# A float32 transformer block on one core: the mixer's triangular inverses in lockstep, its stick-breaking heads in pairs

## The chip, the cores and the metric

One core of a Trainium2 chip runs the whole program. The metric is the time of one execution in microseconds (us) on the device. The engines are PE (TensorE; PEld is its weight load), DVE (VectorE), ACT (ScalarE), POOL (GpSimd) and SP (SyncE, which here only issues DMAs).

## The reference

Two blocks of a model run one after the other on 256 tokens of width 1024, in float32: first attention and a gated feed-forward net, then a hybrid mixer and a mixture of 32 experts. The change lies in the hybrid mixer, which has two branches. One is a gated delta rule over chunks, four heads of 128:

```python
a = jnp.where(strict, jnp.einsum("bhnid,bhnjd->bhnij", k_beta, k) * lmask, 0.0)
m = a + jnp.eye(c, dtype=a.dtype)
u = lax.linalg.triangular_solve(m, v_beta, left_side=True, lower=True, unit_diagonal=True)
w = lax.linalg.triangular_solve(m, k_beta * jnp.exp(decay)[..., None], left_side=True, lower=True, unit_diagonal=True)
...
def step(state, inp):
    qd, kd, uc, wc, qkc, cd = inp
    v_new = uc - jnp.einsum("bhcd,bhde->bhce", wc, state)
    o = jnp.einsum("bhcd,bhde->bhce", qd, state) + jnp.einsum("bhij,bhje->bhie", qkc, v_new)
    state = state * cd[..., None, None] + jnp.einsum("bhcd,bhce->bhde", kd, v_new)
    return state, o
```

The other is stick-breaking attention, eight heads of 64 (each query row sees the 16 meta tokens and the tokens before it):

```python
z = jnp.einsum("bhqd,bhkd->bhqk", q[:, :, s0:s1], k[:, :, :s1]).astype(jnp.float32) * scale
log_keep = jnp.where(mask, jax.nn.log_sigmoid(-z), 0.0)
later = lax.cumsum(log_keep, axis=3, reverse=True) - log_keep
weights = jnp.where(mask, jnp.exp(jax.nn.log_sigmoid(z) + later), 0.0)
outs.append(jnp.einsum("bhqk,bhkd->bhqd", weights.astype(v.dtype), v[:, :, :s1]))
```

Both branches are projected, gated, added and projected again; after a layer norm the experts follow.

## The kernel before

Two kinds of work share PE. The first is the weight stream (class Stream): all dense products of the model in 316 units, in a fixed order. A unit is 128x512 weights, split by ACT into a high part (tiles hiA, hiB) and by DVE into the rest (loA, loB), both in a float32r form, and then 12 products with the high and low parts of the activations (tile fm in the mixer). Up to 7 units are split ahead. Units can have a gate that must be open. The second kind is threads: Python generators for everything that isn't a dense product (attention, norms, the mixer's two branches). All their matmuls are in float32, and each of these leaves two PE instructions; a transpose leaves one.

The order on every engine is written out when the program is built. The function drive() keeps a clock of its own for each engine, with a price for each instruction (classes Queue and TensorQueue, whose calls all have the lines 176, 208 and 213 in the profile). As long as the products issued in the last 0.85 us of that clock hold fewer than WANT = 1000 columns, it takes the next piece of the stream; else the thread whose next step is due; if none is due, the stream again. A stream piece can say that it can't go on (feed() returns False), and the stream then stands until it can. On the chip every engine runs its list in order.

The mixer's part begins at some 380 us. Its threads:

- dn_prep(ci) for the chunks ci = 1, 2 (128 rows) and 0 (16 rows) makes the decays E, the triangular matrix AT, the products PT, and the scaled v and k (vp, ktok).
- dn_inv(ci), one thread for each chunk, inverts the triangular matrix by doubling, in two diagonal blocks of 64 rows for the large chunks: at each level l a masked part am of the matrix (made by POOL), Y = am x (half of the columns), an ACT copy, Z = XD Y, a DVE subtraction from X, and then turned(): four heads' transposes, the lower block by PE's transpose and the upper one by a product with the identity, and an ACT copy to XD. Five levels for the large chunks, three for the small one; at the end one off-diagonal block (YL, Z).
- state_thread runs the three chunks in order (KS, w, Su, QS, PW) when their inverses and preparations are there, and o_thread ends each.
- sb_thread runs the stick-breaking heads. sb_head makes the scores (sz, 64 rows of contraction, 144 and 272 columns), three ACT passes, a DVE pass and two scans, a POOL subtraction, an ACT pass, five transposes (swt), copies; two heads share the products with v (sav). It waits for "sv0" to "sv3", which the stream's value units finish through sv_emit.
- cut_thread starts six loads of expert weights when the heads and the inverses have ended: their tiles lie in the same memory (cut). Nearly all the tiles of both branches are views of it, so the profile calls them cut.

Buffers of limited number are given out by the class Turns: a buffer can be taken when the one taken as many turns before has been given back. d2_turns has 5 (E, dsq, sv, R, w and others); a value unit of the stream waits for one of them (room in win_tiles and fm_tile). When all threads have ended, drive() returns, the mixer's memory is closed, further expert slots are opened, and the stream goes on with the gate br0.

Of the kernel before, what the change touches and what calls it, by code (L numbers as in the profile page):

```python
# [17 lines left out]
D = 1024  # L18
# [29 lines left out]
WANT = 1000.0  # L48
LNS = 1.0
# [131 lines left out]
class TensorQueue:  # L181
# [4 lines left out]
    def __init__(self, clock, engine):  # L186
        self.clock, self.engine, self.now = clock, engine, 0.0
        self.past, self.recent = [], 0.0
# [12 lines left out]
    def matmul(self, out, w, x, **k):  # L201
# [126 lines left out]
def build(tc, I, out):  # L328
# [35 lines left out]
    with ExitStack() as ctx:  # L364
# [62 lines left out]
        d2_turns, z_turns, w_turns, m_turns, p_turns = Turns(5), Turns(3), Turns(2), Turns(3), Turns(2)  # L427
# [1107 lines left out]
        def dn_prep_thread():  # L1535
# [35 lines left out]
            for ci in (1, 2, 0):  # L1571
                spawn(dn_prep(ci))
            spawn(state_thread())
            yield

        def dn_prep(ci):
# [18 lines left out]
            for h in range(4):  # L1595
                T.matmul(p[:C, h * C:(h + 1) * C], kdT[:, h, sl], kdT[:, h, sl], start=True, stop=True)
            X_["AT"] = iv.tile([C, 4, C], F32, name="AT%d" % ci)
            for h in range(4):
                V.scalar_tensor_tensor(X_["AT"][:, h], p[:C, h * C:(h + 1) * C], fb_[:C, ci, h:h + 1], E[:C, h], op0=OP.mult, op1=OP.mult)
            V.tensor_mul(fs[:C, ci], fb_[:C, ci], E[:C, :, C - 1])  # L1600
            if not full:
                d2_turns.give(nE)
            spawn(dn_inv(ci))
            yield
            if full:
                p = acc_tile("kq")
                for h in range(4):
                    T.matmul(p[:C, h * C:(h + 1) * C], kdT[:, h, sl], qdT[:, h, sl], start=True, stop=True)
                X_["PT"] = dm.tile([128, 4, C], F32, name="PT%d" % ci)
                for h in range(4):  # L1610
                    V.scalar_tensor_tensor(X_["PT"][:C, h], p[:C, h * C:(h + 1) * C], fb_[:C, ci, h:h + 1], E[:C, h], op0=OP.mult, op1=OP.mult)
                d2_turns.give(nE)
                yield
            pv = acc_tile("vtp")
            for h in range(4):
                T.transpose(pv[:C, h * 128:(h + 1) * 128], M["raw3"][2][:, h, sl], ident)
            X_["vp"] = (dm if full else iv).tile([128 if full else 16, 4, 128], F32, name="vp%d" % ci)
# [3 lines left out]
            yield  # L1621
            if full:
# [3 lines left out]
                p = acc_tile("qtp")  # L1626
                for h in range(4):
                    T.transpose(p[:C, h * 128:(h + 1) * 128], qdT[:, h, sl], ident)
                for h in range(4):
                    A.activation(sq[:C, h], v4(p)[:C, h], AF.Square, accum_out=fq[:C, ci, h:h + 1])  # L1630
# [6 lines left out]
        def dn_inv(ci):  # L1637

            t0, C = CH[ci]
            X_ = DNC[ci]  # L1640
            AT = X_["AT"]
            K = min(C, 64)
            blocks = [slice(b, b + K) for b in range(0, C, K)]
            L = 4 if C == 16 else 6
            XT = (dm if ci else iv).tile([C, 4, C], F32, name="XT%d" % ci)
            XX = iv.tile([C, 4, K], F32, name="XX%d" % ci)
            bc = lambda t: t[:C, None, :K].to_broadcast([C, 4, K])
            if C > K:
                D_ = iv.tile([C, 4, K], F32, name="AD%d" % ci)
                XD = iv.tile([C, 4, K], F32, name="XD%d" % ci)  # L1650
                for b in blocks:
                    A.copy(D_[b], AT[b, :, b])
                G.memset(XT[K:, :, 0:K], 0.0)
            else:
                D_, XD = AT, XT

            def masked(l):
                am = iv.tile([C, 4, K], F32, name="am%d" % ci, tag="am%d" % ci)
                G.tensor_mul(am, D_, bc(lmask[:, l]))
                return am  # L1660

            def turned():
                p = acc_tile("xt")
                for h in range(4):
                    x = (XX if l else XD)[:, h]
                    T.transpose(p[:K, h * K:(h + 1) * K], x[:K], ident[:K, :K])
                    if C > K:
                        T.matmul(p[K:C, h * K:(h + 1) * K], x[K:], ident[K:C, K:C], start=True, stop=True)
                return v4(p, K)

            l = 0
            yield
            am = masked(0)
            yield
            V.tensor_sub(XD, bc(identc), am)
            am = masked(1)
            yield
            p = turned()
            A.copy(XX, p[:C])
            yield  # L1680
            for l in range(1, L):
                m = 1 << l
                H = K // 2
                xl = XX.rearrange("p h c -> p (h c)").rearrange("p (x u m) -> p x u m", u=2, m=m)[:, :, 0]
                xh = XX.rearrange("p h (x u m) -> p h x u m", u=2, m=m)[:, :, :, 0]
                p = acc_tile("Y")
                for h in range(4):
                    for b in blocks:
                        T.matmul(p[b, h * H:(h + 1) * H], am[b, h], xh[b, h], start=True, stop=True)
                Y = iv.tile([C, 4, H], F32, name="Y%d" % ci, tag="Y%d" % ci)  # L1690
                A.copy(Y, v4(p, H)[:C])
                if l < L - 1:
                    am = masked(l + 1)
                yield
                p = acc_tile("Z")
                for h in range(4):
                    for b in blocks:
                        T.matmul(p[b, h * H:(h + 1) * H], XD[b, h], Y[b, h], start=True, stop=True)
                V.tensor_sub(xl, xl, p[:C, :4 * H].rearrange("p (x m) -> p x m", m=m))
                yield  # L1700
                p = turned()
                if l < L - 1 or C == K:
                    A.copy(XD, p[:C])
                else:
                    A.copy(XT[blocks[0], :, blocks[0]], p[blocks[0]])
                    V.tensor_copy(XT[blocks[1], :, blocks[1]], p[blocks[1]])
                yield
            if C > K:
                lo, hi = blocks
                p = acc_tile("Y")  # L1710
                for h in range(4):
                    T.matmul(p[hi, h * K:(h + 1) * K], AT[lo, h, hi], XX[lo, h], start=True, stop=True)
                Y = iv.tile([C, 4, K], F32, name="YL%d" % ci, tag="am%d" % ci)
                A.copy(Y[hi], v4(p, K)[hi])
                yield
                p = acc_tile("Z")
                for h in range(4):
                    T.matmul(p[lo, h * K:(h + 1) * K], Y[hi, h], XT[hi, h, hi], start=True, stop=True)
                A.mul(XT[lo, :, hi], v4(p, K)[lo], -1.0)
                yield  # L1720
            X_["XT"] = XT
            finish("inv%d" % ci)
# [107 lines left out]
        def sb_thread():  # L1830
            for pr in range(4):
                yield from wait("sv%d" % pr)
                yield from sb_pair(pr)
            finish("sb")

        def sb_head(pr, hh, us):
            skT, sqT = M["skT"], M["sqT"]
            b = hh * 64
            yield from room(z_turns, 2 * pr + hh)
            nz = z_turns.take()  # L1840
            p = a_tile("sz")
            for a in range(2):
                T.matmul(p[:, ZS[a]], sqT[b:b + 64, pr, a * 128:(a + 1) * 128], skT[b:b + 64, pr, :144 + 128 * a],
                         start=True, stop=True)
            z = sw.tile([128, 416], F32, "z", "z%d" % (nz % 3))
            l = sw.tile([128, 416], F32, "l", "l%d" % (nz % 3))
            V.tensor_add(z, p[:, :416], smask)
# [6 lines left out]
            for a in range(2):  # L1854
                r = l[:, ZS[a]][:, ::-1]
                V.tensor_tensor_scan(r, ones.to_broadcast([128, 144 + 128 * a]), r, 0.0, OP.mult, OP.add)
            yield
            G.tensor_sub(z, z, l)
# [3 lines left out]
            yield from room(w_turns, 2 * pr + hh)  # L1862
            nw = w_turns.take()
            pt = acc_tile("swt")
            pt2 = a_tile("swt2")
            for a in range(2):
# [635 lines left out]
```

## Time and profile before

| | |
|---|---|
| time before, median of 3 runs | 861.77 us (850.72, 861.77, 868.59) |
| profiled execution, its own time | 868.72 us |
| its span, first to last instruction | 867.0 us |
| PE, PEld busy | 835.1 us (96%), 693.1 us (80%) |
| DVE, ACT, POOL busy | 489.1 us (56%), 410.5 us (47%), 66.0 us (8%) |
| read from memory | 184.99 MB, 215 GB/s over the span |
| mean granted clock | 0.919 |

The busy time of PE has modelled ends, and matmuls overlap, so the price of one is read from the distance of two starts. Times in the rows are from the span's start. The granted clock is 1.00 at 2.4 GHz and 0.50 at 1.2 GHz.

### The profile page before, as it was taken

How to read it: one execution, taken by the hardware profiler on the slowest of the kernel's cores; microseconds unless marked ns; L12 is line 12 of the kernel's file. 1: busy time of each engine (PE TensorE's matmuls, PEld its weight loads, DVE VectorE, ACT ScalarE, POOL GpSimd, SP SyncE). 2: the span in 40 equal slices, each digit the busy share in tenths (PEclk: the TensorE clock that was granted, in tenths of full speed). 3: DMA queues.
4: the chain of work that ended last, by engine and by line, in shares of the span. 5: the costliest groups of instructions: out<-in, count | busy, mean ns of one | idle time of the engine just before them, and what ended most of it. 6: DMA issues, size and time to landing. Idle time of an engine off the chain costs nothing. (4 is left out here: it accounts for less than half of the span.)

```text
span 867.0 us, 17005 instructions
## 1 busy us (share of the span) xinstructions
PE 835.1 (96%) x6775; PEld 693.1 (80%) x6775; DVE 489.1 (56%) x1245; ACT 410.5 (47%) x903; POOL 66.0 (8%) x99
## 2 busy tenths in 40 slices
PE   8999999999999999999999999999999999998985
PEld 7888899999999999899776767999986555545532
DVE  7676658998788888998332323575655131131104
ACT  6555557765566666766422323575534121222101
POOL 0000001000000002342210101000310000000001
PEclk9999999999999999999855555999999999988998
DMA  8533544474565452754110101399498999999992
GB/s 290 159 117 128 154 147 147 152 239 146 163 226 165 177 195 98 278 164 143 50 49 1 49 1 49 132 410 391 137 340 308 384 423 426 421 425 425 423 403 99
DMA packets 93971, 187.15 MB, mean 216 GB/s; under 512 B 10490, under 2 KB 71219, under 8 KB 82499
## 3 DMA queue, kind: packets, MB, share of 16 engines
q1 hardware_dynamic: 93731, 185.78, 58.6%
q8 instruction: 54, 0.88, 0.4%
q14 instruction: 26, 0.21, 0.1%
q10 hardware_dynamic: 160, 0.27, 0.1%
HBM read 184.99 MB, written 1.05 MB: 215 GB/s over the span
## 5 line engine op out<-in xcount | busy, mean ns | idle before, releaser
L208 PE MATMUL fm<-ah,hiB 128*128 128x256 f32 x268 | 77.4, 289 | 0.0
L208 PE MATMUL fm<-al,hiB 128*128 128x256 f32 x268 | 75.6, 282 | 0.0
L208 PE MATMUL fm<-ah,loB 128*128 128x256 f32 x268 | 75.2, 281 | 0.0
L176 DVE TENSOR_TENSOR hd<-small,ph 128x256 f32<-128x256 f32 x8 | 3.4, 422 | 115.7 <-ACT small L176 115.7
L208 PE MATMUL fm<-hTh,hiB 128*128 128x256 f32 (+1 forms) x184 | 61.2, 333 | 2.0 <-ACT cut L176 1.3
L208 PE MATMUL fm<-ah,hiA 128*128 128x256 f32 x212 | 61.3, 289 | 0.6 <-ACT hiA L176 0.6
L208 PE MATMUL fm<-ah,loA 128*128 128x256 f32 x212 | 59.9, 283 | 0.5 <-DVE loA L176 0.5
L208 PE MATMUL fm<-al,hiA 128*128 128x256 f32 x212 | 59.9, 282 | 0.0
L208 PE MATMUL fm<-hTl,hiB 128*128 128x256 f32 (+1 forms) x184 | 56.4, 307 | 0.0
L208 PE MATMUL fm<-hTh,loB 128*128 128x256 f32 (+1 forms) x184 | 56.4, 306 | 0.0
L208 PEld LDWEIGHTS fm<-ah,hiB 128*128 128x128 f32 x268 | 50.5, 188 | 3.1 <-issue 2.8
L208 PEld LDWEIGHTS fm<-al,hiB 128*128 128x128 f32 x268 | 50.5, 188 | 0.1
L208 PEld LDWEIGHTS fm<-ah,loB 128*128 128x128 f32 x268 | 50.5, 189 | 0.0
L176 ACT ACTIVATE small<-ph 128x256 f32<-128x256 f32 x8 | 3.1, 384 | 95.1 <-PE ph L208 95.1
L208 PE MATMUL fm<-hTh,hiA 128*128 128x256 f32 (+1 forms) x136 | 43.5, 320 | 1.1 <-ACT hiB L176 1.1
L208 PEld LDWEIGHTS fm<-hTh,hiB 128*128 128x128 f32 x184 | 38.1, 207 | 7.3 <-issue 3.6
L176 DVE SCALAR_TENSOR_TENSOR c<-u,pc,c 128x256 f32<-128x256 f32 x88 | 42.5, 483 | 1.8
L208 PEld LDWEIGHTS fm<-ah,hiA 128*128 128x128 f32 x212 | 40.4, 190 | 3.0 <-issue 1.5
L208 PE MATMUL fm<-hTl,hiA 128*128 128x256 f32 (+1 forms) x136 | 41.0, 302 | 0.8 <-DVE hTl L176 0.7
L208 PEld LDWEIGHTS fm<-ah,loA 128*128 128x128 f32 x212 | 40.4, 191 | 0.7 <-DVE loA L176 0.7
L208 PE MATMUL fm<-hTh,loA 128*128 128x256 f32 (+1 forms) x136 | 40.6, 299 | 0.0
L208 PE MATMUL ph<-xg,xe 128*32 128x256 f32 x448 | 38.8, 408 | 1.9 <-DMA xg<-in_expert_w_gate_dram 1.9
(554 smaller groups left out, 2449.6 us busy)
## 6 DMA issues: line engine op xcount, KB each, us to landing
xg<-in_expert_w_gate_dram SPq DMA_DIRECT2D x24, 1024.0 KB, 19.6
xd<-in_expert_w_down_dram SPq DMA_DIRECT2D x18, 1024.0 KB, 19.5
xu<-in_expert_w_up_dram SPq DMA_DIRECT2D x16, 1024.0 KB, 13.9
cut<-in_expert_w_up_dram SPq DMA_DIRECT2D x15, 1024.0 KB, 14.9
wg<-in_ffn_w_up_dram SPq DMA_DIRECT2D x11, 1024.0 KB, 5.1
wu<-in_ffn_w_up_dram SPq DMA_DIRECT2D x11, 1024.0 KB, 4.9
wdn<-in_ffn_w_down_dram SPq DMA_DIRECT2D x11, 1024.0 KB, 5.6
wgt<-in_w_in_dram SPq DMA_DIRECT2D x8, 1024.0 KB
```

What stands on the lines that cost most here:

```text
L176: return f(*args, **k)
L208: return self.engine.matmul(out, w, x, **k)
```

## The change

- The three threads dn_inv become one, inverse_thread. It waits for all three matrices (AT0, AT1, AT2) and copies the diagonal blocks of chunks 1 and 2 into D_, a d2 buffer that it holds to its end. Class Blocks: "J" has eight blocks of 64 for each half of the rows (two chunks, four heads), "0" the 16-row chunk. All levels run in lockstep: Y for all, copies by ACT and DVE, the next mask by DVE, then Z and ZT (the same product transposed, g.y as weights and g.xt moving) and two subtractions, from x and from its transpose xt. Y, Z and ZT have all 64 columns. No transposes are left but the first, a product with the identity.
- dn_prep computes PT in the step of AT, and the q transposes with the v transposes.
- sb_head and the old sb_pair become one thread for two heads: z and l are 2 x 416 wide, the scores of the two heads alternate, ACT's passes and DVE's take both heads at once, the subtraction z - l goes from POOL to DVE. z_turns has 2 pairs, l_turns 1, w_turns 1.
- The planner counts 0.13 us (TURN) for a change between float32 and stream products, 0.0115 for 0.0025 us per stream product, half price for paired scores, and asks for 1300 columns (MIX_WANT) while the mixer's last drive() runs.

```diff
+MIX_WANT = 1300.0
+TURN = 0.13
...
     def run(self, cost, columns, outs, ins):
+        fast = ins[0].dtype != F32
+        if fast != self.fast:
+            cost += TURN
+            self.fast = fast
         self.clock.run(self, cost, outs, ins)
...
-        return self.recent < WANT
+        return self.recent < self.want
...
-            half = 2 if r <= 64 and m <= 64 else 1
+            half = 2 if pair or (r <= 64 and m <= 64) else 1
             self.run(max(n, m) / 600 / half + 0.01, 2 * n * r / 128 / half, [out], [w, x])
         else:
-            self.run(n / 2400 + 0.0025, n * r / 128, [out], [w, x])
+            self.run(n / 2400 + (0.0115 if x.dtype == F32R else 0.0025), n * r / 128, [out], [w, x])
...
-        d2_turns, z_turns, w_turns, m_turns, p_turns = Turns(5), Turns(3), Turns(2), Turns(3), Turns(2)
+        d2_turns, z_turns, l_turns, w_turns, m_turns, p_turns = Turns(5), Turns(2), Turns(1), Turns(1), Turns(3), Turns(2)
...
+            spawn(inverse_thread())
             spawn(state_thread())
...
-        def dn_inv(ci):
...
+        class Blocks:
+            def __init__(self, name, K, halves, n, levels, d):
+                self.K, self.n, self.levels, self.d = K, n, levels, d
+                self.rows = K * halves
+                self.halves = [slice(b * K, (b + 1) * K) for b in range(halves)]
+                self.x, self.xt, self.y = (iv.tile([self.rows, n, K], F32, name=t + name) for t in ("X", "XD", "Y"))
...
+            def mask(self, l):
+                self.am = iv.tile([self.rows, self.n, self.K], F32, name="am" + self.name, tag="am" + self.name)
+                V.tensor_mul(self.am, self.d, self.bc(lmask[:, l]))
+            def each(self, p, w, x):
+                for i in range(self.n):
+                    for b in self.halves:
+                        T.matmul(p[b, i], w[b, i], x(b, i), start=True, stop=True)
+        def inverse_thread():
+            XT = dm.tile([128, 2, 4, 128], F32, name="XT")
+            G.memset(XT[64:, :, :, 0:64], 0.0)
+            lo, hi = slice(0, 64), slice(64, 128)
+            yield from room(d2_turns)
+            nD = d2_turns.take()
+            D_ = d2("D").rearrange("p a (b c) -> p (a b) c", b=2)
+            for ci in (1, 2):
+                yield from wait("AT%d" % ci)
+                for b in (lo, hi):
+                    A.copy(D_[b, 4 * ci - 4:4 * ci], DNC[ci]["AT"][b, :, b])
+            yield from wait("AT0")
+            B = [Blocks("J", 64, 2, 8, 6, D_), Blocks("0", 16, 1, 4, 4, DNC[0]["AT"])]
+            for g in B:
+                g.mask(0)
+            yield
+            P = []
+            for g in B:
+                P.append(g.psum("xt"))
+                g.each(P[-1], g.am, lambda b, i, g=g: identc[b, :g.K])
+            for g, p in zip(B, P):
+                V.tensor_sub(g.xt, g.bc(identc), g.am)
+                g.mask(1)
+                V.tensor_sub(g.x, g.bc(identc), p)
+            yield
+            for l in range(1, 6):
+                P = []
+                for g in B:
+                    P.append(g.psum("Y"))
+                    g.each(P[-1], g.am, lambda b, i, g=g: g.x[b, i])
+                for g, p in zip(B, P):
+                    if g.n == 8:
+                        A.copy(g.y[:, 0:4], p[:, 0:4])
+                        V.tensor_copy(g.y[:, 4:8], p[:, 4:8])
+                    else:
+                        A.copy(g.y, p)
+                    if l < g.levels - 1:
+                        g.mask(l + 1)
                 yield
+                P = []
+                for g in B:
+                    if g.n == 8:
+                        P.append((g.psum("Z"), g.psum("ZT")))
...
+                    g.each(P[-1][0], g.xt, lambda b, i, g=g: g.y[b, i])
+                    g.each(P[-1][1], g.y, lambda b, i, g=g: g.xt[b, i])
+                for g, (pz, pt) in zip(B, P):
+                    V.tensor_sub(g.x, g.x, pz)
+                for g, (pz, pt) in zip(B, P):
+                    if l < 5:
+                        V.tensor_sub(g.xt, g.xt, pt)
...
+            d2_turns.give(nD)
...
+        def sb_pair(pr):
             skT, sqT = M["skT"], M["sqT"]
             nz = z_turns.take()
+            yield from room(l_turns, pr)
+            nl = l_turns.take()
+            z = sw.tile([128, 2, 416], F32, "z", "z%d" % (nz % 2))
+            l = sw.tile([128, 2, 416], F32, "l", "l")
+            P = [a_tile("sz") for hh in range(2)]
             for a in range(2):
+                for hh in range(2):
+                    b = hh * 64
+                    T.matmul(P[hh][:, ZS[a]], sqT[b:b + 64, pr, a * 128:(a + 1) * 128], skT[b:b + 64, pr, :144 + 128 * a],
+                             pair=True, start=True, stop=True)
+            for hh in range(2):
+                V.tensor_add(z[:, hh], P[hh][:, :416], smask)
             yield
             A.activation(l, z, AF.Abs)
             A.activation(l, l, AF.Exp, scale=-1.0)
             A.activation(l, l, AF.Ln, bias=1.0)
             yield
             V.scalar_tensor_tensor(l, z, 0.0, l, op0=OP.max, op1=OP.add)
+            for hh in range(2):
+                for a in range(2):
+                    r = l[:, hh, ZS[a]][:, ::-1]
+                    V.tensor_tensor_scan(r, ones.to_broadcast([128, 144 + 128 * a]), r, 0.0, OP.mult, OP.add)
+            V.tensor_sub(z, z, l)
+            l_turns.give(nl)
...
+        T.want = MIX_WANT
         drive(lambda: not threads and "o2" in done and "sb3" in done)
+        T.want = WANT
```

## Rows read from the trace of the kernel before

**Rows 1.** The page's 40 slices: busy tenths of PE, tenths of the granted clock.

```profile
PE   8999999999999999999999999999999999998985
...
PEclk9999999999999999999855555999999999988998
```

**Rows 2.** Windows view: length, then busy us (instructions) per engine, clock, DMA share, GB/s.

```profile
380.00:425.00 45.00, 43.36 (x383) 39.31 (x381) 33.31 (x99) 26.41 (x91) 9.97 (x18) 1.00 0.38 118
425.00:545.00 120.00, 119.61 (x743) 88.92 (x742) 34.75 (x75) 39.74 (x94) 13.57 (x16) 0.50 0.09 27
545.00:577.00 32.00, 32.00 (x276) 31.13 (x275) 21.62 (x60) 21.89 (x58) 0.00 (x0) 1.00 0.66 264
...
720.00:760.00 40.00, 38.20 (x406) 20.82 (x398) 5.37 (x15) 8.14 (x18) 0.00 (x0) 1.00 1.01 423
```

**Rows 3.** Waits view, 425 to 545 us: who waited for whom, us, times, longest.

```profile
POOL cut L176 <- PE Y L208: 57.8, 8, 15.7
...
PEld Z L208 <- DVE cut L176: 0.7, 2, 0.5
```

**Rows 4.** Timeline of PE at full clock, 411 to 422 us: start, us, instruction.

```profile
411.98 0.24 PE L213 MATMUL xt<-ident,cut 64*64 64x64 f32 x1
...
412.41 0.24 PE L213 MATMUL xt<-ident,cut 64*64 64x64 f32 x1
...
414.50 0.65 PE L208 MATMUL Y<-cut 64*64 64x32 f32 x16
415.08 0.39 PE L208 MATMUL fm<-hTh,hiA 128*128 128x272 f32 x1
...
415.56 0.28 PE L208 MATMUL fm<-hTh,hiA 128*128 128x272 f32 x1
415.68 0.29 PE L208 MATMUL fm<-hTl,hiA 128*128 128x272 f32 x1
...
420.33 0.97 PE L208 MATMUL sz<-cut 64*128 64x144 f32 x4
421.23 0.39 PE L208 MATMUL fm<-hTh,hiA 128*128 128x272 f32 x1
```

**Rows 5.** Timeline at half clock, 440 to 449 us.

```profile
440.95 0.43 PE L208 MATMUL fm<-hTl,hiB 128*128 128x272 f32 x1
...
441.18 0.43 PE L208 MATMUL fm<-hTh,loB 128*128 128x272 f32 x1
...
442.21 1.75 PE L208 MATMUL sz<-cut 64*128 64x144 f32 x4
...
443.90 0.59 PE L208 MATMUL fm<-hTh,hiB 128*128 128x272 f32 x1
...
444.88 0.31 PE L213 MATMUL xt<-ident,cut 64*64 64x64 f32 x1
...
445.52 0.31 PE L213 MATMUL xt<-ident,cut 64*64 64x64 f32 x1
...
447.74 1.06 PE L208 MATMUL Z<-cut 64*64 64x32 f32 x16
...
448.74 0.59 PE L208 MATMUL fm<-hTh,hiB 128*128 128x272 f32 x1
```

**Rows 6.** Groups of PE by shape, 425 to 545 us: busy us, mean ns, idle before.

```profile
L213 PE MATMUL xt<-ident,cut 64*64 64x64 f32 x36 | 11.2, 310 | 0.0
...
L208 PE MATMUL Z<-cut 64*64 64x32 f32 x144 | 9.8, 293 | 0.4 <-DVE cut L176 0.4
L208 PE MATMUL Y<-cut 64*64 64x32 f32 x128 | 8.5, 294 | 0.0
...
L208 PE MATMUL Y<-cut 64*64 64x64 f32 x16 | 2.2, 318 | 0.0
```

**Rows 7.** Groups of DVE by shape, 380 to 577 us.

```profile
L176 DVE TENSOR_TENSOR_SCAN cut<-ones,cut 128x272 f32<-128x272 f32 x8 | 5.6, 699 | 0.0
...
L176 DVE TENSOR_TENSOR loB<-wz,hiB 128x512 fp32r<-128x512 f32 x5 | 3.5, 698 | 0.0
```

More of the change, by code (lines that the diff above doesn't have):

```diff
@@ L1596, in dn_prep @@
                 T.matmul(p[:C, h * C:(h + 1) * C], kdT[:, h, sl], kdT[:, h, sl], start=True, stop=True)
+            if full:
+                p2 = acc_tile("kq")
+                for h in range(4):
+                    T.matmul(p2[:C, h * C:(h + 1) * C], kdT[:, h, sl], qdT[:, h, sl], start=True, stop=True)
             X_["AT"] = iv.tile([C, 4, C], F32, name="AT%d" % ci)
@@ L1599, in dn_prep @@
                 V.scalar_tensor_tensor(X_["AT"][:, h], p[:C, h * C:(h + 1) * C], fb_[:C, ci, h:h + 1], E[:C, h], op0=OP.mult, op1=OP.mult)
+            finish("AT%d" % ci)
             V.tensor_mul(fs[:C, ci], fb_[:C, ci], E[:C, :, C - 1])
[L1601 to L1604, printed above, removed]
             if full:
-                p = acc_tile("kq")
-                for h in range(4):
-                    T.matmul(p[:C, h * C:(h + 1) * C], kdT[:, h, sl], qdT[:, h, sl], start=True, stop=True)
                 X_["PT"] = dm.tile([128, 4, C], F32, name="PT%d" % ci)
                 for h in range(4):
-                    V.scalar_tensor_tensor(X_["PT"][:C, h], p[:C, h * C:(h + 1) * C], fb_[:C, ci, h:h + 1], E[:C, h], op0=OP.mult, op1=OP.mult)
-                d2_turns.give(nE)
-                yield
+                    V.scalar_tensor_tensor(X_["PT"][:C, h], p2[:C, h * C:(h + 1) * C], fb_[:C, ci, h:h + 1], E[:C, h], op0=OP.mult, op1=OP.mult)
+            d2_turns.give(nE)
+            yield
             pv = acc_tile("vtp")
@@ L1616, in dn_prep @@
                 T.transpose(pv[:C, h * 128:(h + 1) * 128], M["raw3"][2][:, h, sl], ident)
+            if full:
+                pq = acc_tile("qtp")
+                for h in range(4):
+                    T.transpose(pq[:C, h * 128:(h + 1) * 128], qdT[:, h, sl], ident)
             X_["vp"] = (dm if full else iv).tile([128 if full else 16, 4, 128], F32, name="vp%d" % ci)
@@ L1625, in dn_prep @@
                 sq = d2("dsq")
[L1626 removed]
                 for h in range(4):
[L1628 to L1630 removed]
+                    A.activation(sq[:C, h], v4(pq)[:C, h], AF.Square, accum_out=fq[:C, ci, h:h + 1])
                 yield
@@ L1861, in sb_head @@
             yield
-            yield from room(w_turns, 2 * pr + hh)
+            yield from room(w_turns, pr)
             nw = w_turns.take()
-            pt = acc_tile("swt")
-            pt2 = a_tile("swt2")
-            for a in range(2):
-                T.transpose(pt2[:16, a * 128:(a + 1) * 128], z[:, 144 * a:144 * a + 16], ident)
-                T.transpose(pt[:, a * 128:(a + 1) * 128], z[:, 144 * a + 16:144 * a + 144], ident)
-            T.transpose(pt[:, 256:384], z[:, 288:416], ident)
@@ L1870, in sb_head @@
-            wt = sw.tile([128, 384], F32, "wt", "wt%d" % (nw % 2))
-            A.copy(wt, pt[:, :384])
-            wm = sw.tile([16, 256], F32, "wm", "wm") if nw % 2 else wm0
-            V.tensor_copy(wm, pt2[:16, :256])
+            pm = a_tile("swm")
+            PT = []
+            for hh in range(2):
+                pt = acc_tile("swt")
+                PT.append(pt)
+                for a in range(2):
+                    T.transpose(pm[:16, hh * 256 + a * 128:hh * 256 + a * 128 + 128], z[:, hh, 144 * a:144 * a + 16], ident)
+                    T.transpose(pt[:, a * 128:(a + 1) * 128], z[:, hh, 144 * a + 16:144 * a + 144], ident)
+                T.transpose(pt[:, 256:384], z[:, hh, 288:416], ident)
@@ L1874, in sb_head @@
+            wt = [sw.tile([128, 384], F32, "wt", "wt%d" % hh) for hh in range(2)]
+            wm = rt_[:16, 0:512]
+            for hh in range(2):
+                A.copy(wt[hh], PT[hh][:, :384])
+            V.tensor_copy(wm, pm[:16])
             z_turns.give(nz)
             yield
-            us.append((hh, wt, wm, nw))
-            if len(us) == 2:
-                av = a_tile("sav")
-                for c in range(3):
-                    for h2, wt, wm, _ in us:
-                        b = h2 * 64
-                        f = (2 * pr + h2) * 64
-                        if c == 0:
-                            T.matmul(av[b:b + 64, :S], M["svm"][:, f:f + 64], wm, start=True, stop=False)
-                        elif c == 1:
-                            T.matmul(av[b:b + 64, :S], M["svt"][:, 0, f:f + 64], wt[:, :S], start=False, stop=False)
-                        else:
-                            T.matmul(av[b:b + 64, 128:S], M["svt"][:, 1, f:f + 64], wt[:, S:], start=False, stop=True)
-                for u in us:
-                    w_turns.give(u[3])
-                oh, ol = M["o"][1]
-                A.copy(oh[:, pr], av[:, :S])
-                yield
-                V.tensor_sub(ol[:, pr], av[:, :S], oh[:, pr].bitcast(F32))
-                finish("sb%d" % pr)
@@ L1897, in sb_pair @@
-        def sb_pair(pr):
-            us = []
-            for hh in range(2):
-                spawn(sb_head(pr, hh, us))
-                yield
+            av = a_tile("sav")
+            for c in range(3):
+                for hh in range(2):
+                    b = hh * 64
+                    f = (2 * pr + hh) * 64
+                    if c == 0:
+                        T.matmul(av[b:b + 64, :S], M["svm"][:, f:f + 64], wm[:, hh * 256:hh * 256 + 256], start=True, stop=False)
+                    elif c == 1:
+                        T.matmul(av[b:b + 64, :S], M["svt"][:, 0, f:f + 64], wt[hh][:, :S], start=False, stop=False)
+                    else:
+                        T.matmul(av[b:b + 64, 128:S], M["svt"][:, 1, f:f + 64], wt[hh][:, S:], start=False, stop=True)
@@ L1903, in build @@
+            w_turns.give(nw)
+            oh, ol = M["o"][1]
+            A.copy(oh[:, pr], av[:, :S])
+            yield
+            V.tensor_sub(ol[:, pr], av[:, :S], oh[:, pr].bitcast(F32))
+            finish("sb%d" % pr)
         stream.open("win")
```

132 lines of the change are left out of this document (36 added, 96 removed).

## The prediction

> **What bounds the kernel now.** I read the page's slices first [rows 1]: TensorE (PE) is busy in nearly every slice, so the share of busy time says nothing; the row to see is the granted clock, which lies at half for five slices in the middle. The windows view puts bounds to it [rows 2]: from 380 to 425 us the clock is full, from 425 to 545 it is 1.2 GHz, then full again. This is the mixer: stick-breaking heads, triangular inverses and their chunks' state, with products of the weight stream put between. In those 120 us PE is busy for 119.6 while VectorE has 34.8 and ScalarE 39.7. The waits say the same [rows 3]: other engines wait for PE, GpSimd 57.8 us for one product, while the largest wait of PE's weight load for VectorE is 0.7 us. So what sets the end of this stage is the length of PE's own queue at the slow clock, not the latency of the chains.
>
> Last, the tail: experts' weights move at 423 GB/s in the window from 720 to 760 us, with the DMA share at 1.01 [rows 2], so the end is a transfer. It doesn't hide the gain: the loads that fill the DMA begin where the mixer gives its buffers back, so the tail moves with the mixer's end. I carry the mixer's gain through at its full size.
>
> **Prices of a PE instruction, at both clocks** (start to start, since matmuls overlap). A product in full float32 leaves two instructions. A stream product takes 0.12 us at full clock (415.56 to 415.68) and 0.23 at half (440.95 to 441.18) [rows 4, 5]: halved. One head's two 64x64 transposes take 0.43 us at full (411.98 to 412.41) and 0.64 at half (444.88 to 445.52). Sixteen instructions of Y or Z, 64x64 by 64x32 with the two halves of the array in turn, take 0.58 (414.50 to 415.08) and 1.00 (447.74 to 448.74). The four scores of a head (sz) take 0.90 (420.33 to 421.23) and 1.69.
>
> **Part 1, the inverses.** Today two chunks of 128 rows each run five levels of Y, Z and a transposition. In the half-clock stretch lie 36 head-turns of 0.64 us, 23.0; 272 Y and Z instructions at 1.00 per 16, 17.0; and the closing products, 16 Y of 64 columns with 2.2 us busy and as many Z, 4.4 [rows 5, 6]. Together 44.4 us. Before 425 lie the other 12 head-turns, 5.2, and 48 instructions, 1.7: 6.9 us. The change removes all transposes and makes Y, Z and a new product ZT, each 64 columns wide: 16 + 16 + 16 products a level for both chunks, five levels, and 16 to start, which makes 256 products, 512 instructions. Their price isn't in the trace as such. If the 64 columns of weights set the pace it is that of today's pairs, 0.58 per 16, 18.6 us; if the 32 moving columns set it, twice that, 37.1. The nearest row decides: the closing Y with 64 moving columns and no partner averages 2.2/16 = 0.14 us at half clock, and two halves side by side make that 1.1 per 16, against the 1.00 measured with 32 columns. So 18.6, with 18.5 more kept for the range. The closing products halve to 2.2. The 16-row chunk has about as many small products as before and is left out. New sum at full clock: 20.8.
>
> **Part 2, the heads in pairs.** The two heads of a pair lie on different halves of the rows, and their scores now alternate between them, so that they can run side by side as Y does. Seven heads in the slow stretch cost 11.8 us, 6.3 at full clock; paired, 3.1. If they don't overlap the gain is nothing; the Y rows exclude that they lose. Transposes and products with v keep their number.
>
> **Part 3, the clock.** What PE did before it fell [rows 2, 4]: groups of 64-column transposes, 1.7 us for four heads, between few stream products. In the changed kernel the transposes are gone, the 64-wide products fill both halves, and the planner asks for more stream columns at a time (MIX_WANT 1300 for 1000) and counts 0.13 us for each change between float32 and stream products. All three push the same way, so I take the clock as held through the mixer. Then what is left of the slow stretch, 119.5 - 44.4 = 75.1, halves to 37.6, less the scores' 3.1: 34.5.
>
> **Part 4, what moves to VectorE.** Masks go from GpSimd to VectorE at twice the width, 0.70 each by the 512-wide row [rows 7]: six of them; five copies of 256 columns, 0.35 each; eleven 512-wide subtractions for ten of 128; the pairs' z minus l, four at 832 columns, 1.1 each. Net some 15 us, on top of the 33.3 + 34.8 + 21.6 = 89.7 that VectorE has from 380 to 577. That is 105 of the 125 us that will be there. In the window 380 to 425 VectorE was already at 74% with PE at 96% [rows 2], so most of it stays beside PE; but masks, subtractions and the weight stream's low halves now stand in one queue, behind a pair's scans, and the inverse's next product waits behind that. I take 8 us of PE waits; nothing is one bound, 34 (below) the other. GpSimd's side is free: its 58 us of waiting was for PE.
>
> **Part 5, the planner's new costs everywhere.** They reorder products outside the mixer too. PE there is at full clock in all but short falls and 9 tenths or more busy [rows 1]; a new order can cost or give some 4 us. I take nothing.
>
> **The sum**, on the profiled execution (868.72; its span is 867.0). From 380 to 577 it used 45.0 + 119.5 + 32.0 = 196.5 us. After: 45.0 - 6.9 - 0.4 (one head's scores) = 37.7; 34.5; 32.0; inverses 20.8: 125.0. Gain 71.5, less 8 of waits, 63.5: 805. The median shown is 861.77 and the runs differ by 18 us, which the length of the slow stretch could explain; if the clock holds, the time after doesn't depend on it, so I keep 805 and not 7 less.
>
> **Rivals.** *The clock still falls.* Then 75.1 - 5.9 = 69.2 stay, the inverses cost 32 groups of 1.00 and 4.4, and there are 37.7 + 69.2 + 36.4 + 32.0 = 175.3: 848. For it: the inverse's products are still 64 by 64, and the clock fell among such products. Against: the three edits above. A fall for part of the stage gives 815 to 848. Chance 0.2.
>
> *The stream locks and the evacuations lie open.* The inverse takes one of five d2 buffers (D_) and holds it to its end; the buffers are handed out in a ring, so after four further takes (two squares, two value tiles sv0 and sv1) the fifth, sv2, must wait, and the stream stands behind it. PE then has only the lockstep, and each of its 13 steps waits for a copy (0.35) or for masks and subtractions (0.7 each), about 1.3 us a step, 17 us, and for a pair's block on VectorE (scans of 832 columns at 0.70 per 272, 2.1, and two passes of 1.1 [rows 7]), 4.3 each, 17 for four: 34. Time 831. For it: the order of the takes in the code. Against: the lockstep may be nearly through when sv2 comes. Chance 0.15. The Trainium skill has a rule that points here: "TensorEngine Tiling (Array Packing)", section Performance Considerations, says that packing speeds up the products but not the emptying of PSUM, which may become the limit. The row of before differs for this stage: there the engine behind waited 57.8 us for PE's Y [rows 3].
>
> *Slower.* Both at once: the lock starves PE at the first levels, the clock falls, and the 34 us open at half clock: 848 + 34 = 882. It is over the 2% from 2.4 us of waiting a step on, at half clock all through. Against it: the dense stream after the lock should raise the clock again, as at 545. Chance 0.04.
>
> *The change doesn't do what it says*: the chains now wait for the slowest chunk, and the removed transposes were only filler. PE's full queue speaks against it; about 862, chance 0.04.
>
> **How the numbers follow.** Forecast 0.57, at 805 (790 to 822). Two per cent is what a measurement of this kernel can tell from no change: 844.5 and 879. Faster: 0.57 + 0.15 + most of the falling clock, 0.13: 0.85. Same 0.11, slower 0.04. Range 786 (no waits, 4 from the order, the rest shrinking by a little more than half) to 846, which takes in the partial falls, the open evacuations and the dear 64-wide products (823).
>
> **What would show it.** Right: a full clock from 380 to the mixer's end, that end near 505, no xt group but the first, 16 J instructions in about 0.6 us, the experts' loads beginning some 65 us sooner. Wrong: a half clock again in that stretch; idle PE in front of Y and Z, with VectorE the releaser; a gap in the stream between sv2 and the end of the inverse. The step that I trust least is the clock.

## The result, and the profile after

The changed kernel takes 822.75 us (median of 4, 819.50 to 829.07); the kernel before beside it 861.84 (4, 850.72 to 868.59). The ratio is 0.960 [0.948, 0.972]: faster, inside the predicted range, but 18 us above the forecast of 805. Some executions of a kernel are slower at a lower granted clock; ratios, and gains over the kernel before, leave these out here and below, so they can differ a little from the quotient of the medians, most for kernels 9 to 11, where this leaves three of the seven executions of before.

The profiled execution of after took 819.50 us, its span is 817.7 and its mean granted clock 0.978. The page's slices, PE's busy tenths and its clock, answer to [rows 1]: the five slices at half clock are gone, but PE is no longer full in the middle.

```profile
PE   8999999999999999999998789999999999998894
...
PEclk9999999999999999999999899999999999989998
```

Windows of after, with the columns of [rows 2]:

```profile
380.00:425.00 45.00, 42.84 (x494) 40.13 (x493) 38.21 (x113) 26.43 (x91) 6.32 (x13) 1.00 0.41 133
425.00:545.00 120.00, 109.11 (x1131) 98.09 (x1132) 76.11 (x161) 62.39 (x132) 0.00 (x0) 0.94 0.37 139
545.00:577.00 32.00, 31.77 (x270) 31.46 (x269) 17.40 (x29) 17.85 (x33) 4.69 (x5) 1.00 0.80 304
...
720.00:760.00 40.00, 37.05 (x309) 20.55 (x310) 5.96 (x10) 6.45 (x13) 0.00 (x0) 0.94 1.01 424
```

From 425 to 545 the clock is 0.94 where it was 0.50, PE has 1131 instructions in place of 743, and VectorE's work has more than doubled, to 76 us. PE is idle for 10.9 us, where it was for 0.4. (The last 16 us of this stretch already belong to br.)

Groups of PE by shape, the first product of the gate br; first the kernel before, then after (shortest, median and longest duration in ns, first and last start in us):

```profile
L208 PE MATMUL br<-od,hiA x32: 277/280/287, 578.4 to 589.6; 128*128 128x256 f32 x32
```

```profile
L216 PE MATMUL br<-od,hiA x32: 277/280/287, 529.3 to 540.4; 128*128 128x256 f32 x32
```

This product starts 49.1 us sooner, and the span is 49.3 us shorter. So the whole gain was made ahead of br, and the tail moved along unchanged: 288.6 us from br to the end before, 288.4 after. The profile of before is of an execution at the slow end of that kernel's times, that of after of its fastest, so the spans lie further apart than the medians (39 us).

PE's timeline of after (start, us, instruction; in brackets idle time and what ended it):

```profile
425.77 0.97 PE L216 MATMUL sz<-cut 64*128 64x144 f32 x8
426.67 0.40 PE L216 MATMUL fm<-hTh,hiA 128*128 128x272 f32 x1
...
444.29 1.15 PE L216 MATMUL Y<-cut 64*64 64x64 f32 x32
445.37 0.65 PE L216 MATMUL sav<-rt,cut 16*64 16x256 f32 x4
...
447.75 1.15 PE L216 MATMUL Z<-cut 64*64 64x64 f32 x32 [0.93 <-ACT cut L179]
448.73 1.10 PE L216 MATMUL ZT<-cut 64*64 64x64 f32 x32
...
453.80 0.28 PE L221 MATMUL swm<-ident,cut 128*16 128x128 f32 x1 [3.97 <-ACT cut L179]
...
455.03 1.97 PE L216 MATMUL Y<-cut 64*64 64x64 f32 x32
```

Both prices of PE work came out. Thirty-two instructions of 64 columns take 1.08 us (444.29 to 445.37) and 0.98 (447.75 to 448.73), 0.49 to 0.54 per 16 where [rows 4] had 0.58 for 32 columns. Two heads' scores take 0.90 (425.77 to 426.67), as one head's did.

From 449.8 to 453.8 PE does nothing. PE's next instructions are a pair's transposes (swm), which wait for ACT's exponential, and this waits for VectorE. First ACT's line, then VectorE's timeline; the inverse's two subtractions, which take Z and ZT, stand behind the same work:

```profile
452.85 0.90 ACT L179 ACTIVATE cut<-cut 128x832 f32<-128x832 f32 x1 [4.88 <-DVE cut L179]
```

```profile
448.67 1.02 DVE L179 SCALAR_TENSOR_TENSOR cut<-cut 128x832 f32<-128x832 f32 x1
449.72 2.04 DVE L179 TENSOR_TENSOR_SCAN cut<-ones,cut 128x144 f32<-128x144 f32 x4
451.79 1.02 DVE L179 TENSOR_TENSOR cut<-cut 128x832 f32<-128x832 f32 x1
452.74 0.68 DVE L179 TENSOR_TENSOR cut<-cut,Z 128x512 f32<-128x512 f32 x1
453.33 0.68 DVE L179 TENSOR_TENSOR cut<-cut,ZT 128x512 f32<-128x512 f32 x1
```

That is the block of a pair which the lock rival described, 4.1 us long against the 4.3 it counted. And the stream gives PE nothing to fill it with. Windows of after for the stream's products (fm) alone, first PE, then PEld, DVE, ACT, and clock, DMA share, GB/s:

```profile
440.00:445.00 5.00, 0.64 (x3) 0.42 (x3) 0.00 (x0) 0.00 (x0) 0.88 0.00 0
445.00:450.00 5.00, 0.00 (x0) 0.00 (x0) 0.00 (x0) 0.00 (x0) 1.00 0.02 3
450.00:455.00 5.00, 0.00 (x0) 0.00 (x0) 0.00 (x0) 0.00 (x0) 0.99 0.00 0
455.00:460.00 5.00, 0.00 (x0) 0.00 (x0) 0.00 (x0) 0.00 (x0) 0.50 0.01 3
460.00:465.00 5.00, 0.00 (x0) 0.00 (x0) 0.00 (x0) 0.00 (x0) 0.83 0.00 0
465.00:470.00 5.00, 3.04 (x18) 2.39 (x18) 0.00 (x0) 0.37 (x1) 1.00 0.65 209
```

No stream product starts from 445 to 465 us. They come back when the inverse ends (its last products start at 464.9) and gives D_ back. The stretch just behind the 4 us of idleness, 455 to 460, is at half clock.

### The profile page after: what moved, and what is told of

Its sections match the earlier page's. It is cut to its first block, busy times and chain, and to the rows that moved or that the text cites. A ratio compares the mean times of both kernels' runs of the same rounds, so it can differ in the third digit from the quotient of the medians.

```text
span 817.7 us, 17080 instructions
## 1 busy us (share of the span) xinstructions
PE 770.6 (94%) x6839; PEld 654.1 (80%) x6839; DVE 501.0 (61%) x1260; ACT 401.5 (49%) x865; POOL 46.8 (6%) x74
## 5 line engine op out<-in xcount | busy, mean ns | idle before, releaser
L216 PE MATMUL fm<-hTh,hiB 128*128 128x256 f32 (+1 forms) x184 | 55.2, 300 | 3.1 <-DVE cv L179 1.4
L216 PE MATMUL fm<-hTl,hiB 128*128 128x256 f32 (+1 forms) x184 | 52.9, 288 | 0.0
L216 PE MATMUL fm<-hTh,loB 128*128 128x256 f32 (+1 forms) x184 | 52.8, 287 | 0.0
L216 PEld LDWEIGHTS fm<-al,hiA 128*128 128x128 f32 x212 | 41.0, 193 | 0.0
L216 PE MATMUL fm<-hTh,hiA 128*128 128x256 f32 (+1 forms) x136 | 40.4, 297 | 0.1
L216 PEld LDWEIGHTS fm<-hTh,hiB 128*128 128x128 f32 x184 | 35.3, 192 | 6.0 <-issue 2.7
L216 PE MATMUL fm<-hTl,hiA 128*128 128x256 f32 (+1 forms) x136 | 38.6, 284 | 0.0
```

## The experiments

Each was timed beside the kernel before, in four groups (1 to 4, 5 to 8, 9 to 11, 12) apart from the whole change, so that across groups the ratios compare better than the times. The table gives the median time (lowest to highest), the ratio to before with its 95% interval, the first start of br and the clock from 425 to 545 us, the last two from the profiled execution. That was the fastest of the four for the whole change, 1 and 10, and the slowest for 3 and 6.

| kernel | us | ratio | br | clock |
|---|---|---|---|---|
| before | 861.84 (850.72 to 868.59) | | 578.4 | 0.50 |
| whole change | 822.75 (819.50 to 829.07) | 0.960 [0.948, 0.972] | 529.3 | 0.94 |
| 1 change, own buffer for D_ | 816.04 (813.68 to 818.36) | 0.949 [0.941, 0.958] | 524.3 | 0.94 |
| 2 inverses alone | 812.21 (808.95 to 818.27) | 0.946 [0.936, 0.955] | 521.7 | 0.97 |
| 3 pairs alone | 849.50 (846.39 to 853.07) | 0.986 [0.977, 0.995] | 564.2 | 0.62 |
| 4 planner alone | 860.05 (833.66 to 894.45) | unclear | 550.5 | 0.86 |
| 5 inverses, own buffer | 811.12 (808.23 to 814.00) | 0.940 [0.935, 0.945] | 520.2 | 0.96 |
| 6 inverses and pairs | 811.11 (810.14 to 813.68) | 0.939 [0.935, 0.943] | 521.6 | 0.93 |
| 7 inverses and planner | 807.99 (807.74 to 808.77) | 0.936 [0.932, 0.940] | 519.7 | 1.00 |
| 8 products beside the transposes | 898.20 (894.00 to 903.24) | 1.039 [1.032, 1.046] | 609.5 | 0.50 |
| 9 turned by products | 808.96 (807.85 to 809.34) | 0.943 [0.932, 0.953] | 520.5 | 0.97 |
| 10 change, 1000 columns | 820.45 (811.83 to 824.38) | 0.958 [0.946, 0.970] | 520.8 | 0.99 |
| 11 change, no turn cost | 805.22 (804.16 to 806.01) | 0.939 [0.928, 0.949] | 515.2 | 0.99 |
| 12 transposes in a row | 814.51 (811.60 to 817.84) | 0.940 [0.934, 0.945] | 528.0 | 0.93 |

**The parts alone (2, 3, 4).** Each takes one part of the diff onto the kernel before.

```diff
 # 2: inverse_thread and Blocks for dn_inv, dn_prep's new order
 # 3: sb_pair for sb_head, its turns, pair=True in the planner
 #    (its low part comes in the same step as the high part; in the change one step later)
 # 4: MIX_WANT, TURN, 0.0115
```

> The kernel before with only the inverses in lockstep (and the preparation's order that goes with it); heads one by one and the planner's numbers as before. Theory: the transposes are what let the clock fall; the half clock between 425 and 545 us shrinks to under 30 us in all, and most of the 39 us comes from this part: 825 to 838. Rival: the planner's larger demand for stream columns holds the clock; then the half clock stays over most of the mixer and only some 20 us of PE work are saved: 840 to 852.

> The kernel before with only the heads in pairs (scores alternating, one thread for two heads; the low part of the result is issued in the same step as the high part); inverses with transposes and the planner's numbers as before. Theory: the clock falls as before, since the transposes are there; the scores lose 5.9 us at half clock: 853 to 862. Rival: the pairs' wider passes free so much that the clock holds: under 840.

> The kernel before with only the planner's numbers (MIX_WANT 1300, TURN 0.13, 0.0115 for each stream product). Theory: transposes still stand in groups of 1.7 us, so the clock still falls in the mixer, perhaps for a shorter time: 845 to 862. Rival: the demand for columns is what holds the clock; then it is full over the mixer with the old inverses, the 119.5 us become some 65 and the time is 810 to 825.

The inverses alone give 812, less than expected and less than the whole change. The pairs alone give 1.4%, 12 us, and not surely 2%. The planner alone is inconclusive: its ten executions lie 60 us apart, and the profiled one (845) is among the faster. The clock tells these apart. Windows of the pairs alone, 425 to 515 us:

```profile
425.00:455.00 30.00, 30.00 (x230) 23.09 (x229) 10.40 (x22) 11.21 (x22) 1.94 (x4) 0.51 0.12 36
455.00:485.00 30.00, 29.83 (x223) 21.70 (x224) 14.03 (x25) 9.32 (x23) 3.19 (x3) 0.60 0.00 1
485.00:515.00 30.00, 30.00 (x194) 21.68 (x195) 9.52 (x18) 10.55 (x22) 0.67 (x1) 0.50 0.12 36
```

Of the kernels that keep the transposes, the pairs' keeps most of the half clock (0.62) and the planner's, in that execution, 34 of 120 us (0.86); with the new inverse it is nearly gone (0.97).

**The lock (1, 5).** The whole change, and the inverses alone, with D_ in memory of its own (that of rt_, whose other use goes back to two tiles of 16 x 256).

```diff
-            yield from room(d2_turns)
-            nD = d2_turns.take()
-            D_ = d2("D").rearrange("p a (b c) -> p (a b) c", b=2)
+            D_ = rt_[:, 0:512].rearrange("p (a c) -> p a c", a=8)
...
-            d2_turns.give(nD)
```

> The changed kernel, with the blocks D_ in memory of their own instead of one of the five d2 buffers (the meta weights wm go back to two tiles of 16x256, so two copies of 256 columns for one of 512). Theory: the ring of d2 buffers stops the stream while the inverse runs; in the changed kernel's trace no stream product lies between 445 and 465 us. Then stream products appear there, the waits of the transposes swm for ACT (4.5 us) and the three short falls of the clock up to 500 us go or shrink, and the time falls by 8 to 16 us against the changed kernel, to 807 to 815. Rival: the lockstep's own hand-overs between PE, ACT and DVE cost the time, whatever stands in the stream: within 3 us of the changed kernel's 822.8.

> The inverses in lockstep alone, with the blocks D_ in a tile of their own, so that the ring of d2 buffers can't stop the stream; old heads, old planner's numbers. In the trace of the inverses alone no stream product lies between 435 and 455 us. Theory: that gap costs as in the changed kernel, where its removal gave some 7 us: 802 to 808. Rival: the stream that isn't issued there only runs later and nothing is lost: 810 to 815.

In the whole change this gives back 6.7 us by the medians, less than the 8 expected at least; the executions don't overlap, the intervals of the ratios do. The same windows of fm show products again where there were none, if not evenly:

```profile
440.00:445.00 5.00, 2.38 (x15) 1.75 (x14) 0.00 (x0) 0.39 (x1) 1.00 0.25 52
445.00:450.00 5.00, 2.01 (x12) 1.60 (x12) 0.00 (x0) 0.30 (x1) 1.00 0.46 161
450.00:455.00 5.00, 0.02 (x1) 0.00 (x0) 0.00 (x0) 0.09 (x1) 0.79 0.01 3
455.00:460.00 5.00, 3.01 (x12) 2.62 (x12) 0.00 (x0) 0.00 (x0) 0.52 0.00 0
```

With the inverses alone the same edit gives 1 us, within the scatter, although the stream stands still there too. So the lock by itself costs nothing that can be measured. That it costs when a pair's block of 4 us falls into it would explain the 6.7 us, but isn't shown: kernel 6 below has the lock and the pairs and takes 811, and kernel 11, the whole change without two of the planner's costs, has the same lock and block and still the lowest median of all. No stream product starts there from 430 to 455 us; its window of fm, and PE's wait for the block:

```profile
430.00:455.00 25.00, 0.00 (x0) 0.00 (x0) 0.00 (x0) 0.00 (x0) 0.93 0.01 2
```

```profile
443.18 0.28 PE L221 MATMUL swm<-ident,cut 128*16 128x128 f32 x1 [3.48 <-ACT cut L179]
```

**Two parts at a time (6, 7).**

```diff
 # 6: the whole change without MIX_WANT, TURN and 0.0115
 # 7: the whole change with the old sb_head and its turns
```

> Inverses in lockstep and heads in pairs, old planner's numbers: the changed kernel without its planner part. The inverses alone gave 812.2, the whole change 822.8; something in the other two parts costs 10 us. If it is the planner's numbers: 806 to 813 here. If it is the pairs: 818 to 825.

> Inverses in lockstep and the planner's new numbers, heads one by one: the changed kernel without its pairs. If the planner's numbers cost the 10 us: 818 to 826. If it is the pairs: 808 to 814.

Either addition leaves the inverses' time as it was within the scatter, 811 and 808. Only all three together cost 11 to 15 us more by the times, and the ratios agree (0.960 against 0.939 and 0.936, with intervals that don't overlap). So it is the pairs and the planner's numbers that collide.

**Which number of the planner (10, 11).**

```diff
-MIX_WANT = 1300.0      # 10
+MIX_WANT = 1000.0
-TURN = 0.13            # 11
+TURN = 0.0
-... (0.0115 if x.dtype == F32R else 0.0025)
+... (0.0025 if x.dtype == F32R else 0.0025)
```

> The whole change, with the planner asked for 1000 stream columns in the mixer as before, not 1300. Theory (more stream products between the lockstep's steps make the inverse end later and the stream's buffers run out while it waits; together with the pairs' blocks on VectorE that is the 10 to 15 us that the whole change lies above its parts): 808 to 815, and the inverse ends before 462 us (465 in the whole change). Rival (the cost of a turn between float32 and stream products moves the order, not the wanted columns): 818 to 826, as the whole change.

> The whole change, with the planner's two new costs taken back (no 0.13 us for a turn between float32 and stream products, 0.0025 us on each stream product), the 1300 columns kept. Theory of the wanted columns: no change, 818 to 826. Rival (the costs): 808 to 815. If both this and the kernel with 1000 columns come out at 818 or above, the meeting of pairs and planner is one of order alone and stays open.

It is the costs, not the columns: without them the change takes 805.2, its four executions within 2 us, and its ratio is that of kernel 6, which has none of the planner's numbers. With 1000 columns the median stays at 820; the profiled execution of that kernel was its fastest, 811.8, so its row in the table doesn't stand for the median. My theory of the columns fell. The windows from 380 to 515 us, first of the whole change, then of the kernel without turn costs:

```profile
380.00:515.00 135.00, 122.31 (x1376) 108.77 (x1375) 98.85 (x247) 71.92 (x190) 6.32 (x13) 0.95 0.24 77
```

```profile
380.00:515.00 135.00, 126.37 (x1470) 115.02 (x1470) 101.81 (x249) 79.37 (x204) 4.34 (x9) 0.99 0.35 122
```

PE is idle for 8.6 us instead of 12.7, and the clock is 0.99 instead of 0.95, another 5.4 us of PE's time (0.04 of 135). That is 9.5 of the 14.1 us by which br starts sooner. In the other executions of the whole change the clock weighs more: its four mean clocks are 0.964 to 0.978, those of kernel 11 0.983 to 0.985. By an estimate (span times what the mean clock lacks to 1) the half clock costs 24 us on average in the one and 13 in the other, 11 of the 17.5 us between them. Why the costs leave such an order with pairs and not with single heads stays open.

**What lets the clock fall (8, 9, 12).** All three are the kernel before with an edit in turned(). Kernel 8 puts two wide products behind each head's turn; they are additional, the planner doesn't count them, and nothing uses what they compute. Kernel 9 turns the lower block as the upper one always was, by a product with the identity. Kernel 12 has the same instructions as before, but a group's four transposes first and then its four products.

```diff
 # 8, behind each head's turn
+                        for i in range(2):
+                            T.engine.matmul(f[:, :256], identr, hTh[:, h, 0:256], start=True, stop=True)
 # 9
-                    T.transpose(p[:K, h * K:(h + 1) * K], x[:K], ident[:K, :K])
+                    T.matmul(p[:K, h * K:(h + 1) * K], x[:K], ident[:K, :K], start=True, stop=True)
 # 12, between transpose and product
+                for h in range(4):
+                    x = (XX if l else XD)[:, h]
```

> The kernel before, with two dummy stream-form products (128x128 weights, 256 columns, result unused) behind each head's transposes in the large chunks' inverses: 96 more products, 11 us of PE at full clock, 22 at half. Theory: the clock fell because the transposes' groups are thin; with dense products between them it stays up for much of the mixer, and half of 120 us is far more than 11: 820 to 845. Rival: the gain of the change is the removed PE work, not the clock: the half clock stays and the time rises by 10 to 22 us, 872 to 885.

> The kernel before, with one operation exchanged: the lower block of each head is turned by a product with the identity, as the upper one already is, and no longer by PE's transpose. Theory (what made the old inverse dear is the change between transposes and products inside a group): a head-turn falls from 0.43 us to some 0.15 at full clock, the clock holds at least for most of the stage, and the time comes to 812 to 832, most of what the new inverse alone gave (812). Rival (the clock fell because the old inverse is many small groups with narrow products, whatever turns them): the head-turns get cheaper, 48 x 0.28 = 13 us at full clock and 36 x 0.4 of them at half, but the half clock stays for most of the stage: 845 to 858. Rival 2: a product with the identity is no cheaper: 862.

> The kernel before, with a group's four transposes of the lower block issued one behind the other and then the four products of the upper block, where they alternated. PE's instructions are the same. Theory (the change between transpose and product on PE is the price, at 0.17 to 0.25 us each way): four heads' turns fall from 1.72 us to some 0.8 at full clock, since seven of eight changes go, and the clock holds for most of the mixer: 809 to 825. Rival (a 64x64 transpose is dear by itself): a group stays over 1.3 us, the half clock stays: 850 to 866. Between: the groups get cheaper but the clock still falls for the stage: 835 to 850.

Kernel 8 went the wrong way, by 35 us, beyond the rival's range too: the theory that dense products put between hold the clock fell in this form. Kernel 9 is one line, and at 809 (none over 809.4) it gives more than the whole change (none under 819.5). Kernel 12 gives 814.5 from an exchange of order alone. Timelines of the same group of four heads, in kernel 8 (its first head), 9 and 12:

```profile
411.93 0.24 PE L213 MATMUL xt<-ident,cut 64*64 64x64 f32 x1
412.10 0.32 PE L208 MATMUL xt<-ident,cut 64*64 64x64 f32 x2
412.36 0.51 PE L1671 MATMUL fill<-hTh,identr 128*128 128x256 f32 x2
412.79 0.24 PE L213 MATMUL xt<-ident,cut 64*64 64x64 f32 x1
```

```profile
412.17 0.68 PE L208 MATMUL xt<-ident,cut 64*64 64x64 f32 x16
412.78 0.50 PE L213 MATMUL svt<-ident,sv 128*16 128x128 f32 x3
```

```profile
411.81 0.41 PE L213 MATMUL xt<-ident,cut 64*64 64x64 f32 x4
412.14 0.67 PE L208 MATMUL xt<-ident,cut 64*64 64x64 f32 x8
412.75 0.50 PE L213 MATMUL svt<-ident,sv 128*16 128x128 f32 x3
```

L213 is the transpose, L208 the product. Alternating, the group took four times the 0.43 of [rows 4], 1.72 us. In a row it takes 0.94 (411.81 to 412.75): 0.33 for the four transposes and 0.61 for the products. By products alone it takes the same 0.61 for twice as many, so the lower block's run beside the upper one's. The work isn't dear, then, the changes are: three round trips between transpose and product less save 0.78, 0.26 each, or 0.20 each if the change that is left costs nothing. In kernel 8 a head keeps its round trip and adds 0.43 of products.

With the changes went the half clock. Windows of kernel 12:

```profile
425.00:455.00 30.00, 30.00 (x373) 24.20 (x373) 19.65 (x40) 16.48 (x42) 8.76 (x10) 1.00 0.12 37
455.00:485.00 30.00, 29.61 (x289) 23.21 (x288) 13.85 (x30) 17.59 (x41) 4.88 (x4) 0.88 0.24 71
485.00:515.00 30.00, 30.00 (x226) 27.16 (x226) 15.81 (x47) 15.06 (x43) 1.07 (x1) 0.83 0.33 123
```

That is 17 us at half clock (0.12 and 0.17 of 30, twice) in place of about 119, from an order of eight steps within a group.

Two rules of the Trainium skill bear on this. "Perfetto Trace Analysis", section Transposes, asks that a logical transpose be done as a transpose and not as a standard matmul: here the runs differ, and the exchange the other way is worth 49 us. "TensorE: Matmul & The Clock Gate", Part 4: PE-mode transpose, says that the full clock doesn't engage for transposes: kernel 12 has all of them and runs at full clock but for 17 us of this stretch, so their number alone doesn't decide.

## Why the prediction was right or wrong

**The bound: right.** PE's queue at half clock set the mixer's length. A kernel that gives PE cheaper turns and the full clock by one line (9) gains 49 us.

**Part 1, the inverses: right in both prices.** The turns are gone, and 64 columns cost 0.49 to 0.54 per 16, for 0.58; the upper bound of 1.16 was far off.

**Part 2, the scores: right**, halved. The pairs alone gave 12 us, more than the 3 from this at full clock or 5.9 at half; the half clock was also less (0.62 for 0.50).

**Part 3, the clock: right in direction, short in size and wrong in its reasons.** I had three edits push together. One is enough: no alternation of transposes and products. Without it the pairs (3) don't hold the clock and the planner (4) does only in part, and with it neither is needed (9). The costs of the planner don't even push that way: beside the pairs the clock is higher without them (11). It did not hold quite through: 0.94 over 120 us is 7 us of PE's time that I had not counted.

**Part 4, the waits: the term was mis-sized.** From 380 to 527.8 us PE was idle for 12.7 us, and for 2.0 in the same stage before; 10.7 where I took 8. The lock came as the rival had it, to the buffer and the 4 us block. But its 34 us were far too many: of the four blocks that it counted one shows in full as idle PE, the 4.0 us above (in front of the pair's transposes with ACT the releaser, not of Y or Z), giving D_ its own buffer returned 6.7, and kernel 11 has lock and block at 805. The 57.8 us that I set beside the lock as the wait of the engine behind are GpSimd's, which makes the masks and empties no PSUM; in the same view ACT waits 11.0 us for Y and VectorE 20.2 for Z, so that PE was the limit stands.

**Part 5, the planner: right outside the mixer, and the term that was missing inside it.** "I take nothing", with 4 either way, holds where I applied it: the first transposes of k (ktp) start at 386.5 us before and 386.6 after, and the tail is the same to 0.2. (There PE was not always 9 tenths busy, as I wrote: the first and three of the last four slices of [rows 1] are lower.) Inside the mixer I counted the planner only as a help to the clock. There its two costs made the whole change 17.5 us slower than it is without them (822.75 against 805.22), mostly through the half clock, the rest through idleness and what I can't assign. The shortfall of 14.2 us between the forecast gain of 63.5 and the 49.3 of the profiled spans is 2.7 of waits, 7 of clock, and some 4.5 unassigned; it is almost the 14.1 us by which br starts sooner without the costs. So the sum, and its 805, describe kernel 11: br starts there 63.2 us sooner than before. That its 8 us for waits agree is in part luck: in kernel 11 they are 6.6 us more idleness and 1.4 of clock.

**The tail moved along: right**, to 0.2 us. The rivals of a clock that stays down, of a slower kernel and of pure filler are out; the time lies nearest to the lock's 831, but by the planner's costs beside the pairs, and the lock's part in it isn't shown.

## What to carry to other kernels

When TensorE is busy throughout and yet at half clock, look at what alternates in its queue before rebuilding the algorithm: here one line, or one exchange of order, gave what the rebuild gave. Time parts of a change alone and in twos; two parts that are harmless each beside the third cost 11 to 15 us together. A planner's more detailed cost isn't a better order until it is timed with the work that it orders.

## What the hardware showed that was not expected

- Where a 64x64 transpose in full float32 alternates with a 64x64 product on the other half of the array, the change there and back costs 0.20 to 0.26 us; the eight turns of a group take 0.61 us as products.
- The clock stood at half for 120 us with PE idle for 0.4 of them [rows 2]; as the ends of PE's instructions are modelled, waiting inside the alternation would not show as idle. Undoing the alternation in 12 groups of eight turns ended it but for 7 us (kernel 9) or 17 (kernel 12). What in the alternation does this, the time it takes or the change of mode, was not separated.
- In full float32, 64 moving columns cost no more than 32 behind 64 columns of weights: 0.49 to 0.54 us per 16 against 0.58.
